# A rotary embedding on one core: the first batch's stores issued later, and one GpSimd product per tile

## The chip, the cores and the metric

The kernel runs on one core of a Trainium2 chip. Times are device microseconds of a whole execution; the profile's span (first to last instruction) is 1.8 to 2.5 us shorter. Engines: DVE is VectorE, POOL is GpSimd, ACT is ScalarE, PE is TensorE, SP issues the loads, ACT also issues the stores. "Transfer engines" are the 16 DMA engines that all loads and stores of the core share.

## The reference

```python
# x: (8, 2048, 8, 64) fp32; cos, sin: (2048, 32) fp32
x1 = x[..., :32]
x2 = x[..., 32:]
out1 = x1 * cos - x2 * sin          # cos, sin broadcast over batch and heads
out2 = x1 * sin + x2 * cos
return np.concatenate([out1, out2], axis=-1)
```

There are 33.55 MB to read, 33.55 MB to write, and 0.52 MB of tables.

## The kernel before

A batch is 4.19 MB. It lies in SBUF as 128 partitions of 8192 values (16 positions of 8 heads of 64), is changed in place and stored. There are five such buffers for eight batches, so batch 5's load waits until batch 0 is stored. A tile is mostly 2048 values per partition, a quarter of a batch.

```python
def store(b, lo, n):
    keep(nc.scalar.dma_start(out=ov[b, :, lo : lo + n], in_=xts[b][:, lo : lo + n]))

for b in range(NBUF):            # 5
    load(b)
# ... identity matrices, nsin = -sin, copies of the tables to PSUM

def rotate(b, lo, n):
    # ... views; kind is "A" (DVE adds), "B" (PE adds), "C" (PE adds, DVE makes both products)
    if kind != "C":
        for u, tab in ((1, sin_sb), (0, nsin)):
            keep(nc.gpsimd.tensor_mul(           # two products per tile, half a tile each
                out=t2u[:, :, u, :].rearrange("p (r h) d -> p r h d", h=H),
                in0=xu[:, :, 1 - u, :].rearrange("p (r h) d -> p r h d", h=H),
                in1=rep(tab[:, r0 : r0 + nr, :], H)))
    keep(nc.vector.tensor_mul(out=t1..., in0=xk, in1=rep(cos_ps[...], 2 * H)))
    if kind == "A":
        keep(nc.vector.tensor_add(out=xt, in0=t1, in1=t2))
    # ... "B", "C": two matmuls with the identity per 512 columns, ACT copies the sum back to xt

for b in range(B):
    # ...
    for lo, n in spans(pieces(b)):
        rotate(b, lo, n)
        # ... once the batch is complete in program order:
                if b == 0:
                    for part in spans([HD, HD, 2 * HD, UNIT, 2 * UNIT]):
                        store(b, *part)          # each waits only for its own tiles
                else:
                    store(b, *whole)
    if b + NBUF <= last:
        load(b + NBUF)
```

Of the kernel before, what the change touches and what calls it, by code (L numbers as in the profile page):

```python
# [9 lines left out]
@with_exitstack  # L10
def kernel(
    ctx: ExitStack,
    tc: tile.TileContext,
    x: bass.AP,
    cos: bass.AP,
    sin: bass.AP,
    out: bass.AP,
):
    nc = tc.nc
    keep = tc.keep_in_program_order  # L20
    f32 = mybir.dt.float32
    PSUM = bass.MemoryType.PSUM

    B, S, H, D = x.shape
    Dh = D // 2
    P = 128
    HD = H * D
    R = S // P
    ROW = R * HD
    UNIT = 4 * HD  # L30
    NBUF = 5
    C = 512
    last = B - 1

    xv = x.rearrange("b (q r) h d -> b q (r h d)", q=P)
    ov = out.rearrange("b (q r) h d -> b q (r h d)", q=P)
    cos_src = cos.rearrange("(q r) d -> q r d", q=P)
    sin_src = sin.rearrange("(q r) d -> q r d", q=P)

    const_pool = ctx.enter_context(tc.tile_pool(name="const", bufs=1))  # L40
    tab_pool = ctx.enter_context(tc.tile_pool(name="tab", bufs=1, space=PSUM))
    t1_pool = ctx.enter_context(tc.tile_pool(name="t1p", bufs=1, space=PSUM))
    o_pool = ctx.enter_context(tc.tile_pool(name="op", bufs=2, space=PSUM))
    t1s_pool = ctx.enter_context(tc.tile_pool(name="t1s", bufs=2))
    xpool = ctx.enter_context(tc.tile_pool(name="xpool", bufs=NBUF))
    t2_pool = ctx.enter_context(tc.tile_pool(name="t2p", bufs=3))

    cos_sb = const_pool.tile([P, R, Dh], f32, tag="cb")
    sin_sb = const_pool.tile([P, R, Dh], f32, tag="sb")
    nsin = const_pool.tile([P, R, Dh], f32, tag="ns")  # L50
    eye = const_pool.tile([P, P], f32, tag="eye")
    neye = const_pool.tile([P, P], f32, tag="neye")
    cos_ps = tab_pool.tile([P, R, Dh], f32, tag="cp")
    sin_ps = tab_pool.tile([P, R, Dh], f32, tag="sp")

    xts = {}

    def spans(sizes):
        lo = 0
        for n in sizes:  # L60
            yield lo, n
            lo += n

    def load(b):
        xt = xpool.tile([P, ROW], f32, tag="xt", name=f"xt{b}")
        for lo, n in spans([UNIT, UNIT, 2 * UNIT] if b == 0 else [ROW]):
            keep(nc.sync.dma_start(out=xt[:, lo : lo + n], in_=xv[b, :, lo : lo + n]))  # L67
            if b == 0 and lo == 0:
                keep(nc.sync.dma_start(out=cos_sb, in_=cos_src))  # L69
                keep(nc.sync.dma_start(out=sin_sb, in_=sin_src))  # L70
        xts[b] = xt

    def store(b, lo, n):
        keep(nc.scalar.dma_start(out=ov[b, :, lo : lo + n], in_=xts[b][:, lo : lo + n]))

    for b in range(NBUF):
        load(b)

    nc.gpsimd.memset(eye, 0.0)  # L79
    nc.gpsimd.affine_select(  # L80
        out=eye,
        in_=eye,
        compare_op=mybir.AluOpType.not_equal,
        fill=1.0,
        base=0,
        pattern=[[-1, P]],
        channel_multiplier=1,
    )
    keep(nc.scalar.mul(nsin, sin_sb, -1.0))  # L89
    keep(nc.scalar.copy(sin_ps, sin_sb))  # L90
    keep(nc.scalar.mul(neye, eye, -1.0))
    keep(nc.vector.tensor_copy(cos_ps, cos_sb))  # L92

    def rep(a, n):
        return dataclasses.replace(a, ap=[a.ap[0][:], a.ap[1][:], [0, n], a.ap[-1][:]])

    kinds = {}
    for b, kind in ((1, "C"), (2, "B"), (3, "C"), (4, "B"), (5, "B")):
        kinds[(b, 0)] = kind

    def rotate(b, lo, n):
        kind = kinds.get((b, lo), "A")
        xt = xts[b][:, lo : lo + n]
        r0 = lo // HD
        nr = n // HD
        xk = xt.rearrange("p (r k d) -> p r k d", r=nr, d=Dh)
        xu = xt.rearrange("p (g u d) -> p g u d", u=2, d=Dh)
        if kind == "A":
            t1 = t1_pool.tile([P, n], f32, tag="t1")
        else:  # L110
            t1 = t1s_pool.tile([P, n], f32, tag="t1s")
        if kind == "C":
            t2 = t1s_pool.tile([P, n], f32, tag="t1s")
        else:
            t2 = t2_pool.tile([P, n], f32, tag="t2")
        t1u = t1.rearrange("p (g u d) -> p g u d", u=2, d=Dh)
        t2u = t2.rearrange("p (g u d) -> p g u d", u=2, d=Dh)
        if kind != "C":
            for u, tab in ((1, sin_sb), (0, nsin)):
                keep(  # L120
                    nc.gpsimd.tensor_mul(  # L121
                        out=t2u[:, :, u, :].rearrange("p (r h) d -> p r h d", h=H),
                        in0=xu[:, :, 1 - u, :].rearrange("p (r h) d -> p r h d", h=H),
                        in1=rep(tab[:, r0 : r0 + nr, :], H),
                    )
                )
        keep(
            nc.vector.tensor_mul(  # L128
                out=t1.rearrange("p (r k d) -> p r k d", r=nr, d=Dh),
                in0=xk,  # L130
                in1=rep(cos_ps[:, r0 : r0 + nr, :], 2 * H),
            )
        )
        if kind == "A":
            keep(nc.vector.tensor_add(out=xt, in0=t1, in1=t2))  # L135
        elif kind == "B":
            for j in range(n // C):
                o = o_pool.tile([P, C], f32, tag="o")
                cs = slice(j * C, (j + 1) * C)
                nc.tensor.matmul(o, eye, t1[:, cs], start=True, stop=False)  # L140
                nc.tensor.matmul(o, eye, t2[:, cs], start=False, stop=True)  # L141
                keep(nc.scalar.copy(xt[:, cs], o))  # L142
        else:
            keep(
                nc.vector.tensor_mul(  # L145
                    out=t2.rearrange("p (r k d) -> p r k d", r=nr, d=Dh),
                    in0=xk,
                    in1=rep(sin_ps[:, r0 : r0 + nr, :], 2 * H),
                )
            )  # L150
            G = C // Dh
            for u in range(2):
                for j in range(n // 2 // C):
                    o = o_pool.tile([P, C], f32, tag="o")
                    gs = slice(j * G, (j + 1) * G)
                    nc.tensor.matmul(o, eye, t1u[:, gs, u, :], start=True, stop=False)  # L156
                    nc.tensor.matmul(  # L157
                        o, eye if u else neye, t2u[:, gs, 1 - u, :], start=False, stop=True
                    )
                    keep(  # L160
                        nc.scalar.copy(  # L161
                            xu[:, gs, u, :], o.rearrange("p (g d) -> p g d", d=Dh)
                        )
                    )

    def pieces(b):
        if b == 0:
            return [2 * HD, 2 * HD, UNIT, UNIT, UNIT]
        if b == last:
            return [UNIT, UNIT, UNIT, 2 * HD, 2 * HD]  # L170
        return [UNIT] * 4

    for b in range(B):
        done = 0
        outs = list(spans([2 * UNIT, UNIT, UNIT] if b == last else [ROW]))
        for lo, n in spans(pieces(b)):
            rotate(b, lo, n)
            done = lo + n
            while outs and sum(outs[0]) <= done:
                whole = outs.pop(0)  # L180
                if b == 0:
                    for part in spans([HD, HD, 2 * HD, UNIT, 2 * UNIT]):
                        store(b, *part)
                else:
                    store(b, *whole)
        if b + NBUF <= last:
            load(b + NBUF)


# [28 lines left out]
```

## Time and profile before

| | before |
|---|---|
| time, median of 6 runs | 163.95 us (163.52 to 164.19) |
| span of the profiled run | 161.9 us |
| DVE, POOL busy | 140.1 us (87%), 139.0 us (86%) |
| moved | 67.6 MB, mean 418 GB/s over the span |
| DVE's last add ends | 152.46 us |

In the page's slice rows each character is one fortieth of the span and its digit the busy share in tenths. The chain of waits follows the last instruction back and attributes the span by engine. The stretches table has the DMA share and GB/s in its last two columns; over a few microseconds its GB/s scatter widely, so for short stretches this text sums single packet records, each packet's bytes spread evenly over its duration. The lines themselves stand in the prediction below.

### The profile page before, as it was taken

The page shows a single profiled execution, that of the slowest core. Times are in us where ns is not written, and L with a number is a line of the kernel's source. Part 1 is how long each engine was busy: PE and PEld are TensorE (multiplying, and loading weights), DVE is VectorE, ACT ScalarE, POOL GpSimd, SP SyncE. Part 2 cuts the span into 40 slices and gives each one's busy share as a digit, 9 for nine tenths or more (in the row PEclk, how much of TensorE's full clock was granted, in tenths as well). Part 3 has the DMA queues.
Part 4 walks back from the last instruction along what each step waited for, and adds up shares of the span by engine and source line. Part 5 has one row for each costly group of instructions (what it writes and reads, how often), then busy time and mean ns, then how long its engine had stood idle before and what let it go on. Part 6 is the DMA issues. An engine that isn't in the chain of part 4 may idle for free.

```text
span 161.9 us, 470 instructions
## 1 busy us (share of the span) xinstructions
PE 46.7 (29%) x80; PEld 18.6 (11%) x80; DVE 140.1 (87%) x66; ACT 14.4 (9%) x24; POOL 139.0 (86%) x70
## 2 busy tenths in 40 slices
PE   0000000498009950893039903970000000000000
PEld 0000000142004310340023402320000000000000
DVE  0468999999999999999999999999999999999600
ACT  3300000014000220041001210130000000000000
POOL 1299999999999899999994999999999999996000
PEclk9999999999955796599755985899555555555555
DMA  5999999999998989998999999989999999999994
GB/s 188 417 435 505 438 413 413 413 421 437 437 470 344 465 364 445 494 413 389 510 397 389 518 391 397 502 389 407 494 397 413 486 397 421 478 397 409 429 417 178
DMA packets 3746, 67.65 MB, mean 418 GB/s; under 512 B 416, under 2 KB 416, under 8 KB 1056
## 3 DMA queue, kind: packets, MB, share of 16 engines
q1 hardware_dynamic: 1728, 34.08, 49.6%
q10 hardware_dynamic: 2016, 33.56, 48.3%
q14 instruction: 2, 0.02, 0.0%
HBM read 34.08 MB, written 33.55 MB: 418 GB/s over the span
## 4 chain that ended last, share of the span: by engine, by line
DVE 75%; POOL 9%; issue 6%; DMA 3%; SPq 0%; DVEq 0%; POOLq 0%
DVE t L128 40%; DVE xt L135 33%; POOL t L121 9%; DMA sin_sb<-in_sin_dram 3%; DVE t L145 3%; DVEq L135 0%; SPq L69 0%; SPq L67 0%; POOLq L121 0%
## 5 line engine op out<-in xcount | busy, mean ns | idle before, releaser
L121 POOL TENSOR_TENSOR t<-xt,sin_sb 128x1024 f32<-128x1024 f32 (+1 forms) x32 | 71.1, 2222 | 8.6 <-DMA sin_sb<-in_sin_dram 5.6
L128 DVE TENSOR_TENSOR t<-xt,cos_ps 128x2048 f32<-128x2048 f32 (+1 forms) x34 | 73.4, 2167 | 0.8
L121 POOL TENSOR_TENSOR t<-xt,nsin 128x1024 f32<-128x1024 f32 (+1 forms) x32 | 71.2, 2225 | 0.0
L135 DVE TENSOR_TENSOR xt<-t,t 128x2048 f32<-128x2048 f32 (+1 forms) x29 | 62.2, 2145 | 5.4 <-POOL t L121 2.5
L140 PE MATMUL o<-t,eye 128*128 128x512 f32 x24 | 17.1, 804 | 25.0 <-DVE t L128 25.0
L156 PE MATMUL o<-t,eye 128*128 128x512 f32 x16 | 10.9, 786 | 36.6 <-DVE t L128 36.6
L141 PE MATMUL o<-t,eye 128*128 128x512 f32 x24 | 15.2, 719 | 0.0
L142 ACT COPY xt<-o 128x512 f32<-128x512 f32 x12 | 7.0, 586 | 46.5 <-PE o L141 46.5
L140 PEld LDWEIGHTS o<-t,eye 128*128 128x128 f32 x24 | 5.6, 250 | 33.4 <-issue 33.4
L161 ACT COPY xt<-o 128x512 f32<-128x512 f32 x8 | 4.7, 586 | 42.7 <-DVE t L128 26.6
L156 PEld LDWEIGHTS o<-t,eye 128*128 128x128 f32 x16 | 3.6, 248 | 41.5 <-POOL t L121 30.4
L141 PEld LDWEIGHTS o<-t,eye 128*128 128x128 f32 x24 | 6.0, 251 | 8.5 <-issue 8.5
L92 DVE COPY cos_ps<-cos_sb 128x512 f32<-128x512 f32 x1 | 0.7, 695 | 6.1 <-DMA cos_sb<-in_cos_dram 6.1
L157 PE MATMUL o<-t,neye 128*128 128x512 f32 x8 | 4.9, 722 | 0.2 <-DVE t L145 0.2
L145 DVE TENSOR_TENSOR t<-xt,sin_ps 128x2048 f32<-128x2048 f32 x2 | 4.6, 2280 | 0.0
L157 PE MATMUL o<-t,eye 128*128 128x512 f32 x8 | 4.1, 592 | 0.0
L157 PEld LDWEIGHTS o<-t,neye 128*128 128x128 f32 x8 | 1.8, 239 | 3.7 <-issue 3.7
L157 PEld LDWEIGHTS o<-t,eye 128*128 128x128 f32 x8 | 1.5, 190 | 1.9 <-issue 1.9
L89 ACT ACT_TABLE_LOAD x1 | 1.3, 1283 | 0.7 <-PEq L202 0.7
L89 ACT ACTIVATE nsin<-sin_sb 128x512 f32<-128x512 f32 x1 | 0.6, 630 | 4.8 <-DMA sin_sb<-in_sin_dram 4.8
L90 ACT COPY sin_ps<-sin_sb 128x512 f32<-128x512 f32 x1 | 0.6, 579 | 0.0
L79 POOL MEMSET eye<- 128x128 f32 x1 | 0.2, 205 | 0.3 <-POOLq L202 0.3
(6 smaller groups left out, 1.0 us busy)
## 6 DMA issues: line engine op xcount, KB each, us to landing
xt<-in_x_dram SPq DMA_DIRECT2D x7, 4096.0 KB, 26.7
out_dram<-xt ACTq DMA_DIRECT2D x6, 4096.0 KB, 33.3
out_dram<-xt ACTq DMA_DIRECT2D x2, 2048.0 KB, 24.3
out_dram<-xt ACTq DMA_DIRECT2D x3, 1024.0 KB, 11.2
xt<-in_x_dram SPq DMA_DIRECT2D x2, 1024.0 KB, 5.9
xt<-in_x_dram SPq DMA_DIRECT2D x1, 2048.0 KB, 11.4
out_dram<-xt ACTq DMA_DIRECT2D x2, 256.0 KB, 18.9
out_dram<-xt ACTq DMA_DIRECT2D x1, 512.0 KB, 32.6
```

What stands on the lines that cost most here:

```text
L89: keep(nc.scalar.mul(nsin, sin_sb, -1.0))
L92: keep(nc.vector.tensor_copy(cos_ps, cos_sb))
L121: nc.gpsimd.tensor_mul(out=t2u[:, :, u, :].rearrange("p (r h) d -> p r h d", h=H), in0=xu[:, :, 1 - u, :].rearrange("p (r h) d -> p r h d" ...
L128: nc.vector.tensor_mul(out=t1.rearrange("p (r k d) -> p r k d", r=nr, d=Dh), in0=xk, in1=rep(cos_ps[:, r0 : r0 + nr, :], 2 * H),)
L135: keep(nc.vector.tensor_add(out=xt, in0=t1, in1=t2))
L140: nc.tensor.matmul(o, eye, t1[:, cs], start=True, stop=False)
L141: nc.tensor.matmul(o, eye, t2[:, cs], start=False, stop=True)
L142: keep(nc.scalar.copy(xt[:, cs], o))
L145: nc.vector.tensor_mul(out=t2.rearrange("p (r k d) -> p r k d", r=nr, d=Dh), in0=xk, in1=rep(sin_ps[:, r0 : r0 + nr, :], 2 * H),)
L156: nc.tensor.matmul(o, eye, t1u[:, gs, u, :], start=True, stop=False)
L157: nc.tensor.matmul(o, eye if u else neye, t2u[:, gs, 1 - u, :], start=False, stop=True)
L161: nc.scalar.copy(xu[:, gs, u, :], o.rearrange("p (g d) -> p g d", d=Dh))
```

## The change

There are two intents. The first batch's stores should not compete with the loads of batches 1 to 4, and POOL should be relieved: one product of a whole tile, through a view that swaps the halves and a table that holds -sin and sin side by side, in place of two products of half a tile. The sine and cosine tables move into a rotating buffer to make room.

```diff
--- before.py
+++ after.py
@@ -45,9 +45,9 @@
     xpool = ctx.enter_context(tc.tile_pool(name="xpool", bufs=NBUF))
     t2_pool = ctx.enter_context(tc.tile_pool(name="t2p", bufs=3))
 
-    cos_sb = const_pool.tile([P, R, Dh], f32, tag="cb")
-    sin_sb = const_pool.tile([P, R, Dh], f32, tag="sb")
-    nsin = const_pool.tile([P, R, Dh], f32, tag="ns")
+    cos_sb = t1s_pool.tile([P, R, Dh], f32, tag="t1s", name="cos_sb")
+    sin_sb = t1s_pool.tile([P, R, Dh], f32, tag="t1s", name="sin_sb")
+    sgn = const_pool.tile([P, R, 2, Dh], f32, tag="sg")
     eye = const_pool.tile([P, P], f32, tag="eye")
     neye = const_pool.tile([P, P], f32, tag="neye")
     cos_ps = tab_pool.tile([P, R, Dh], f32, tag="cp")
@@ -86,13 +86,27 @@
         pattern=[[-1, P]],
         channel_multiplier=1,
     )
-    keep(nc.scalar.mul(nsin, sin_sb, -1.0))
+    for lo, hi in ((0, 4), (4, R)):
+        keep(nc.scalar.mul(sgn[:, lo:hi, 0, :], sin_sb[:, lo:hi, :], -1.0))
+        keep(nc.scalar.copy(sgn[:, lo:hi, 1, :], sin_sb[:, lo:hi, :]))
     keep(nc.scalar.copy(sin_ps, sin_sb))
     keep(nc.scalar.mul(neye, eye, -1.0))
     keep(nc.vector.tensor_copy(cos_ps, cos_sb))
 
     def rep(a, n):
         return dataclasses.replace(a, ap=[a.ap[0][:], a.ap[1][:], [0, n], a.ap[-1][:]])
+
+    def swapped(a, nr):
+        return dataclasses.replace(
+            a,
+            offset=a.offset + Dh,
+            ap=[a.ap[0][:], [HD, nr], [D, H], [-Dh, 2], [1, Dh]],
+        )
+
+    def signed(a, nr):
+        return dataclasses.replace(
+            a, ap=[a.ap[0][:], [D, nr], [0, H], [Dh, 2], [1, Dh]]
+        )
 
     kinds = {}
     for b, kind in ((1, "C"), (2, "B"), (3, "C"), (4, "B"), (5, "B")):
@@ -116,14 +130,13 @@
         t1u = t1.rearrange("p (g u d) -> p g u d", u=2, d=Dh)
         t2u = t2.rearrange("p (g u d) -> p g u d", u=2, d=Dh)
         if kind != "C":
-            for u, tab in ((1, sin_sb), (0, nsin)):
-                keep(
-                    nc.gpsimd.tensor_mul(
-                        out=t2u[:, :, u, :].rearrange("p (r h) d -> p r h d", h=H),
-                        in0=xu[:, :, 1 - u, :].rearrange("p (r h) d -> p r h d", h=H),
-                        in1=rep(tab[:, r0 : r0 + nr, :], H),
-                    )
+            keep(
+                nc.gpsimd.tensor_mul(
+                    out=t2.rearrange("p (r h u d) -> p r h u d", r=nr, h=H, u=2),
+                    in0=swapped(xt, nr),
+                    in1=signed(sgn[:, r0 : r0 + nr, :, :], nr),
                 )
+            )
         keep(
             nc.vector.tensor_mul(
                 out=t1.rearrange("p (r k d) -> p r k d", r=nr, d=Dh),
@@ -178,12 +191,14 @@
             done = lo + n
             while outs and sum(outs[0]) <= done:
                 whole = outs.pop(0)
-                if b == 0:
+                if b == 1:
                     for part in spans([HD, HD, 2 * HD, UNIT, 2 * UNIT]):
-                        store(b, *part)
-                else:
+                        store(0, *part)
+                if b > 0:
                     store(b, *whole)
-        if b + NBUF <= last:
+        if b == 1:
+            load(NBUF)
+        if b > 0 and b + NBUF <= last:
             load(b + NBUF)
```

## The prediction

> **What bounds the kernel now.** I read the page from the top: busy shares, slices, transfer queues, and the chain of waits last, because three things are near their limit at once (DVE, POOL and the DMA engines) and a chain can name only one.
>
> ```profile
> span 161.9 us, 470 instructions
> PE 46.7 (29%) x80; PEld 18.6 (11%) x80; DVE 140.1 (87%) x66; ACT 14.4 (9%) x24; POOL 139.0 (86%) x70
> ...
> DVE  0468999999999999999999999999999999999600
> ...
> POOL 1299999999999899999994999999999999996000
> ...
> DMA  5999999999998989998999999989999999999994
> ...
> HBM read 34.08 MB, written 33.55 MB: 418 GB/s over the span
> ...
> DVE 75%; POOL 9%; issue 6%; DMA 3%; SPq 0%; DVEq 0%; POOLq 0%
> ```
>
> The busy shares (87% and 86%) and the chain (DVE 75%) tempt one to call this a DVE and POOL kernel. The slices say otherwise: the DMA row is the only one that is full from the second slice to the last but one, while DVE and POOL stop some 10 us before the end. So I looked at the end, first in the timeline, then in the table of stretches:
>
> ```profile
> 142.58 10.25 ACTq L74 DMA_DIRECT2D out_dram<-xt  x3
> 151.23 1.23 DVE L135 TENSOR_TENSOR xt<-t,t 128x1024 f32<-128x1024 f32 x1
> 152.49 0.34 ACTq L74 DMA_DIRECT2D out_dram<-xt  x1
> ```
>
> ```profile
> 4.00:37.00 33.00, 6.38 (x10) 2.49 (x11) 28.13 (x15) 2.50 (x5) 30.11 (x16) 1.00 1.03 439
> 37.00:57.00 20.00, 10.92 (x19) 4.42 (x18) 19.48 (x10) 2.37 (x5) 19.53 (x9) 0.74 0.98 411
> 62.00:122.00 60.00, 27.32 (x48) 11.12 (x48) 58.25 (x27) 7.04 (x12) 57.48 (x26) 0.73 1.01 436
> 122.00:158.00 36.00, 0.00 (x0) 0.00 (x0) 29.39 (x15) 0.00 (x0) 26.23 (x14) 0.50 0.99 426
> 158.00:161.90 3.90, 0.00 (x0) 0.00 (x0) 0.00 (x0) 0.00 (x0) 0.00 (x0) 0.50 0.40 170
> ```
>
> The last two columns are the DMA share and GB/s. The last add ends at 152.46 us and the last 1.05 MB store is issued at 152.49, yet the span ends at 161.9. I summed the trace's single packet records (each packet's bytes spread over its duration) to see what the engines did meanwhile: 3.08 MB moved after 152.5, at 429 GB/s. So 3.08 - 1.05 = 2.03 MB of earlier stores stood in the queue ahead of it, worth 2.03 / 0.43 = 4.7 us. The same sums show the rate at 431 to 433 GB/s from 10.6 to 44 us, a dip between 44 and 58 (395 to 430), and again 429 to 433 from 58 to 159. Nothing is left idle: **the kernel is bound by moving 67.6 MB**. Check: 67.6 / 0.432 = 156.5 us, plus 2.2 us until transfers run, plus about 1.3 for slower small packets up to 8 us and the dip, plus 1.9 us from the last packets (160.0) to the end = 161.9.
>
> **What the Trainium skill says.** "DMA: Bandwidth & Descriptors", section "Where 436 GB/s comes from", gives 435.2 GB/s for the 16 ports of a core together; the 432 to 433 here agree, so the rate cannot rise. The same page, "Queues, rings and completion order", says that an engine takes turns between queues packet by packet. The trace agrees: from 20 to 30 us loads moved 4.08 MB and stores 0.24, because a row of a load is 32 KB in one packet and the first store parts have 2 KB and 4 KB packets. "GPSIMD Engine Reference", section 3.1, has 4497 ns for a two-input product of 2048 fp32 elements, and 2293 ns on DVE. DVE agrees (2292 ns). POOL's row here is for 1024 elements:
>
> ```profile
> L121 POOL TENSOR_TENSOR t<-xt,nsin 128x1024 f32<-128x1024 f32 x28 | 66.1, 2360 | 0.0
> L121 POOL TENSOR_TENSOR t<-xt,sin_sb 128x1024 f32<-128x1024 f32 x28 | 66.0, 2356 | 3.1 <-DVE xt L135 2.6
> L135 DVE TENSOR_TENSOR xt<-t,t 128x2048 f32<-128x2048 f32 x25 | 57.3, 2292 | 3.8 <-POOL t L121 1.2 <-DVE t L128 0.4
> ```
>
> Two of these are 4.72 us by their records, but they overlap: in the timeline they start every 2.28 us (18.58, 20.86, 23.15, 25.43), so a pair takes 4.57 us of POOL. Section 7 of that page warns of inner steps over 8 bytes; the new operands keep an inner step of 4 bytes, so nothing there speaks of a penalty.
>
> **The change part by part.**
>
> *One product for two.* POOL goes from 64 products to 32: 28 of 2048 and 4 of 1024 elements, 28 + 2 = 30 tiles' worth. Each replaces 4.57 us by an estimated 4.5 (the skill's figure; the trace has no such instruction), so POOL loses about 30 x 0.07 = 2 us of work. None of it is on the path: DVE needs two passes per ordinary tile, which in the timeline start 4.72 us apart, POOL 4.57, and DVE waited for POOL only 2.5 us in all. Even a shorter DVE chain would not move the end, by the first part. Worth 0 us.
>
> *The table.* ACT now makes four small pieces in place of one 0.63 us negation, and POOL's first product waits for two of them. The 128x128 negation of the identity took 0.30 us, starting 0.5 us after an operation four times as wide, so two 128-column pieces cost about 0.55 us: POOL starts near 7.4 us, not 6.89, and DVE's first add slips by some 0.4 us. DVE's end goes to about 152.9. The slack there is 4.7 us. Worth 0 us.
>
> *The first batch's stores later.* ACT issued five parts (4.19 MB) between 10.66 and 28.5 us. The order of instructions after the change has them behind the four ACT copies of batch 1's first tile, which ended at 40.5 us before. So from 11 to 40 us only loads run. By 40.5 us they have moved some 16.4 MB instead of 15.6, a gain in loads of just the 0.8 MB that stores lose. The fifth load (batch 4) also no longer waits for a store part, but four loads were queued ahead of it. Its end moves from 57.6 to perhaps 54 us.
> The next load (batch 5) waits until all of batch 0 is stored. In both kernels this is when five loads, the tables and one store, 21.5 + 4.2 = 25.7 MB, have moved: 2.2 + 25.7 / 0.43 = 62 us (before: the store was done at 62.7). From there the queues hold the same work in both. All of it comes earlier than DVE needs it: batch 5's load ended at 84.5 and DVE took it up at 97.4. DVE waited for no load of x in batches 1 to 7. What can change is the 0.54 us that the dip from 44 to 58 us cost (0.234 MB missing against 432 GB/s): its small packets now meet other loads. From -0.5 to +0.5 us, centre -0.1.
>
> *Tables in the t1s buffers.* They are read by 9 us; their first reuse is at 28. Worth 0.
>
> Sum: 163.98 + 0 + 0 - 0.1, rounded to **163.8 us**.
>
> **The rivals.**
> 1. *POOL becomes the bound.* The operands now have four free dimensions, one with a negative step, which no instruction of the trace has. POOL would end at 7.4 + 30 x T plus few waits; it ended at 148.2 and DVE 4.2 us later. The end moves once DVE ends later than 152.5 + 4.7 = 157.2, so POOL after 153, or T above 4.85 us (6% over 4.57). At T = 5.2 the time would be some 173 us. Against it: the old operands were already runs of 32 elements with a repeated table, at practically the skill's rate for plain ones. I give it 5%.
> 2. *A dry transfer queue.* Stores held back could leave the engines idle once loads wait for buffers. At about 54 us the loads run out, but then 3.5 MB of batch 0 and 4.2 of batch 1 (issued at 46.7) are queued, 18 us of work, and load 5 enters at 62. Were it wrong, each idle us is a us of time. Under 5%.
> 3. *Engine-bound reading.* If the chain were right (DVE and POOL bound), 2 us off POOL or earlier loads would show as 1 to 3 us: 161 to 163. Against it stand the 2 MB queued when DVE ends.
> 4. *Pure loads run faster than the mix.* 430 GB/s at 8 to 10.6 us against 431.8 after: they don't.
>
> **Range and chances.** The three runs before span 0.7 us. Adding the dip's 0.5 either way: 163.0 to 164.9. Faster by over 2% (below 160.7) would need more than 435 GB/s or the ends to shrink: 1%. Slower by over 2% (above 167.3) is rivals 1 and 2: 6%. Within 2%: 93%.
>
> **What would show it.** Right: DMA full from the second slice to the last but one, mean 416 to 420 GB/s; the last DVE add between 152 and 154 us and the span near 162; POOL's product near 4.5 us; batch 5's load issued at 61 to 63 us. Wrong: a POOL mean above 4.85 us with DVE waiting on it; a DMA slice below 9 inside; or a span under 160 with DVE's last add earlier by as much.

## The result, and the profile after

| | before | after |
|---|---|---|
| time, median of 6 runs | 163.95 us | 164.05 us (163.81 to 164.71) |
| span of the profiled run | 161.9 us | 162.1 us |
| DVE, POOL busy | 140.1, 139.0 us | 140.1, 135.8 us |
| DVE's last add ends | 152.46 us | 153.15 us |
| batch 0 stored; batch 4 loaded (by the bytes moved; the last packet ends up to 0.4 us later) | 62.7; 57.6 us | 63.0; 53.6 us |
| last transfer packet ends | 160.6 us | 160.7 us |

The ratio of after to before is 1.0014, 95% interval 0.9989 to 1.0038.

The page after, the same parts as of before:

```profile
span 162.1 us, 440 instructions
PE 48.0 (30%) x80; PEld 19.3 (12%) x80; DVE 140.1 (86%) x66; ACT 15.1 (9%) x27; POOL 135.8 (84%) x38
...
DVE  0459899999999999999999899999999999999700
...
POOL 1199999999999799999994989999999999994000
...
DMA  5999999999999899998999999999999999999994
...
HBM read 34.08 MB, written 33.55 MB: 417 GB/s over the span
...
DVE 74%; POOL 8%; issue 7%; DMA 3%; SPq 0%; DVEq 0%; ACT 0%
```

POOL is relieved by some 3 us and the span does not move. The DMA row is as full as before (two slices show an 8, four did before); what the engines do under it was rearranged. The groups of POOL and DVE after (count, then busy us and mean ns, then idle us before them and its cause):

```profile
L134 POOL TENSOR_TENSOR t<-xt,sgn 128x2048 f32<-128x2048 f32 x28 | 125.9, 4526 | 5.1 <-DVE xt L148 5.1
L148 DVE TENSOR_TENSOR xt<-t,t 128x2048 f32<-128x2048 f32 x25 | 57.3, 2292 | 3.9 <-DVE t L141 0.9 <-POOL t L134 0.9
```

Start to start, undisturbed whole products are 4.47 to 4.50 us apart, against 4.57 for a pair before. What POOL saves returns as waiting: it idled 5.1 us for DVE, 2.6 before. The end of the timeline after:

```profile
143.27 10.25 ACTq L74 DMA_DIRECT2D out_dram<-xt  x3
...
151.92 1.23 DVE L148 TENSOR_TENSOR xt<-t,t 128x1024 f32<-128x1024 f32 x1
153.18 0.34 ACTq L74 DMA_DIRECT2D out_dram<-xt  x1
```

DVE's end is 0.69 us later than before, and the transfers end at the same time all the same.

### The profile page after: what moved, and what is told of

It is laid out like the page before. It is cut to its first block, busy times and chain, and to the rows that moved or that the text cites. A ratio compares the mean times of both kernels' runs of the same rounds, so it can differ in the third digit from the quotient of the medians.

```text
span 162.1 us, 440 instructions
## 1 busy us (share of the span) xinstructions
PE 48.0 (30%) x80; PEld 19.3 (12%) x80; DVE 140.1 (86%) x66; ACT 15.1 (9%) x27; POOL 135.8 (84%) x38
## 4 chain that ended last, share of the span: by engine, by line
DVE 74%; POOL 8%; issue 7%; DMA 3%; SPq 0%; DVEq 0%; ACT 0%
DVE t L141 40%; DVE xt L148 32%; POOL t L134 8%; DMA sin_sb<-in_sin_dram 3%; DVE t L158 3%; DVEq L148 0%; SPq L69 0%; SPq L67 0%; ACT sgn L90 0%; ACT sgn L91 0%
## 5 line engine op out<-in xcount | busy, mean ns | idle before, releaser
L134 POOL TENSOR_TENSOR t<-xt,sgn 128x2048 f32<-128x2048 f32 (+1 forms) x32 | 135.1, 4253 | 11.4 <-ACT sgn L91 6.3
L170 PE MATMUL o<-t,neye 128*128 128x512 f32 x8 | 6.1, 882 | 0.1
L170 PEld LDWEIGHTS o<-t,neye 128*128 128x128 f32 x8 | 2.5, 329 | 4.8 <-issue 4.8
L90 ACT ACTIVATE sgn<-sin_sb 128x128 f32<-128x128 f32 (+1 forms) x2 | 0.8, 415 | 5.0 <-DMA sin_sb<-in_sin_dram 5.0
L91 ACT COPY sgn<-sin_sb 128x128 f32<-128x128 f32 (+1 forms) x2 | 0.8, 388 | 0.0
```

What stands on the lines that cost most here:

```text
L90: keep(nc.scalar.mul(sgn[:, lo:hi, 0, :], sin_sb[:, lo:hi, :], -1.0))
L91: keep(nc.scalar.copy(sgn[:, lo:hi, 1, :], sin_sb[:, lo:hi, :]))
L134: nc.gpsimd.tensor_mul(out=t2.rearrange("p (r h u d) -> p r h u d", r=nr, h=H, u=2), in0=swapped(xt, nr), in1=signed(sgn[:, r0 : r0 + nr, ...
L170: nc.tensor.matmul(o, eye if u else neye, t2u[:, gs, 1 - u, :], start=False, stop=True)
```

## The experiments

Theory T: moving the bytes binds, and DVE's end has some 4 us to spare. Rival D: the DVE and POOL chain, which carries 82 to 84% of the chain of waits (DVE alone 74 to 75%), binds.

### More work on DVE: e1 and e2

The changed kernel with a cosine product of batch 6 made a second time, for one tile (e1) or all four (e2); the results stay right.

```diff
+        if b == 6 and lo // UNIT in (1,):        # e2: (0, 1, 2, 3)
+            keep(nc.vector.tensor_mul(out=t1..., in0=xk, in1=rep(cos_ps[...], 2 * H)))
         if kind == "A":
```

e1, one more product:

> The changed kernel with one of DVE's cosine products of batch 6 made twice (2.3 us more DVE work, same result). Theory T (transfers bind, DVE's end has some 4 us to spare): last add ends near 155.4 us instead of 153.15, span and time stay within 0.4 us of the changed kernel (164.05). Rival D (the DVE and POOL chain binds): time 2.3 us up, 166.3.

e2, four more:

> The changed kernel with all four cosine products of batch 6 made twice (9.2 us more DVE work). T: last add near 162.3 us; the stores ahead of the last one would be drained by 157.6 (160.0 less 2.4 for 1.05 MB), so 4.4 us of the 9.2 are hidden and the rest shows, plus 0 to 2 us for starting on an empty queue: time 168.8 to 171. D: all 9.2 us show, 173.3.

Measured: e1 164.10 us (163.92 to 164.58), ratio to before 1.0012 (0.9957 to 1.0066); e2 169.08 us (168.97 to 169.14), ratio 1.031. The timelines' ends, e1 first, then e2:

```profile
154.12 1.22 DVE L156 TENSOR_TENSOR xt<-t,t 128x1024 f32<-128x1024 f32 x1
155.38 0.34 ACTq L74 DMA_DIRECT2D out_dram<-xt  x1
```

```profile
152.34 10.25 ACTq L74 DMA_DIRECT2D out_dram<-xt  x3
...
160.99 1.22 DVE L156 TENSOR_TENSOR xt<-t,t 128x1024 f32<-128x1024 f32 x1
```

In e1 DVE ends 2.2 us later than in the changed kernel and the time does not follow. In e2 it ends at 162.21, 9.06 us later, and the time rises by 5.0 (over e1's of the same rounds, too): 4.1 us were hidden, about the 4.4 expected. D, which wanted 2.3 and 9.2 us, falls. The stretches of e2 show the spare time used up: from 140 to 144 us, while batch 6 was still being worked on, the queue ran dry. In the packet records it was empty once more from 161 to 163 us, before the last store.

```profile
130.00:140.00 10.00, 0.00 (x0) 0.00 (x0) 9.79 (x5) 0.00 (x0) 9.34 (x3) 0.50 0.97 419
140.00:144.00 4.00, 0.00 (x0) 0.00 (x0) 3.86 (x3) 0.00 (x0) 1.45 (x2) 0.50 0.33 139
```

### Fewer bytes: e3, e4 and e5

e3 is the changed kernel without the last quarter of batch 4's store, e4 without all of it; e5 is the kernel before without all of it. Their results are wrong in the places not stored.

```diff
# e3
+                if b == 4:
+                    store(b, 0, 3 * UNIT)
-                if b > 0:
+                elif b > 0:
                     store(b, *whole)
# e4
-                if b > 0:
+                if b > 0 and b != 4:
                     store(b, *whole)
# e5
-                else:
+                elif b != 4:
                     store(b, *whole)
```

e3, 1.05 MB less:

> The changed kernel without the last quarter of batch 4's store (1.05 MB less; result wrong on purpose in that quarter). T: 1.05 MB at 432 GB/s is 2.4 us: time 161.6, and DVE's last add stays at 153.1. D: no change, 164.0.

e4, 4.19 MB less, changed kernel:

> The changed kernel without batch 4's store (4.19 MB less; result wrong on purpose in that batch). T: 9.7 us of transfer vanish, but then the last store waits for DVE's end at 153.1 us, so only the spare 4 us less 0 to 1.5 us for an empty queue are gained: time 160 to 162, bound by DVE now. D: no change, 164.0.

e5, 4.19 MB less, kernel before:

> The kernel before without batch 4's store, to see the change where DVE binds. T: DVE's last add ends at 152.5 us here and 0.7 us later with the change, so this is 0.7 us (0.4 to 1.0) faster than the changed kernel without that store: 159.3 to 161.3. D, with POOL's 2 us on the path: the changed one is up to 2 us faster.

Measured: e3 161.63 us, 2.42 below the changed kernel's 164.05 and 2.37 below e6 (164.00, next section but one), which ran on the same chip in the same rounds, as 1.05 MB at 432 GB/s would have it. e4 160.16 (159.72 to 160.34) and e5 159.39 (159.19 to 159.57), same chip and rounds. Without the 4.19 MB only about 4 us are gained in place of 9.7, because then DVE is the bound. The DMA rows of e4 and, second, e5 show the holes:

```profile
DMA  5999999999999999999999999999999990997946
```

```profile
DMA  5999999999999999999999999999999990997946
```

And here, where the engines' work does count, the change costs: the medians differ by 0.77 us, and DVE's last add ends at 153.26 us in e4 and 152.55 in e5, 0.71 later (its line in e4, then in e5):

```profile
152.03 1.23 DVE L148 TENSOR_TENSOR xt<-t,t 128x1024 f32<-128x1024 f32 x1
```

```profile
151.32 1.23 DVE L135 TENSOR_TENSOR xt<-t,t 128x1024 f32<-128x1024 f32 x1
```

POOL's shorter work gives nothing even then, since DVE waited for POOL hardly at all after the start (in the changed kernel 2.7 us in all, 2.5 of them in batch 0); the later start of POOL comes through to DVE's end in full. The first instructions, before and then after, show where it begins (start us, duration us):

```profile
6.77 0.63 ACT L89 ACTIVATE nsin<-sin_sb 128x512 f32<-128x512 f32 x1 [4.75 <-DMA sin_sb<-in_sin_dram]
...
6.89 1.26 POOL L121 TENSOR_TENSOR t<-xt,sin_sb 128x512 f32<-128x512 f32 x1 [5.58 <-DMA sin_sb<-in_sin_dram]
```

```profile
7.03 0.31 ACT L90 ACTIVATE sgn<-sin_sb 128x128 f32<-128x128 f32 x1 [5.02 <-DMA sin_sb<-in_sin_dram]
7.25 0.28 ACT L91 COPY sgn<-sin_sb 128x128 f32<-128x128 f32 x1
...
7.61 2.35 POOL L134 TENSOR_TENSOR t<-xt,sgn 128x1024 f32<-128x1024 f32 x1 [6.31 <-ACT sgn L91]
```

Before, POOL began with the sine as it came from memory; after, it waits for two pieces from ACT and starts 0.72 us later. Of this 0.26 us is the sine landing later in that run. In all 14 traces POOL begins 0.12 us after ACT's first work on the sine with two products, and 0.58 with one: the new table costs 0.46 us. That work itself begins between 6.77 and 7.13 us, whichever kernel runs, and this scatter is the rest (7.13 in e4 and 6.87 in e5: again 0.26). What makes up the rest of the 0.77 between the medians is not shown.

### The parts one by one: e6 and e7

e6 is the kernel before with the later stores alone, e7 with the single product and its table alone (each takes its half of the diff above).

e6, stores late:

> The kernel before with only the later issue of batch 0's stores. T: the queues hold the same work from 63 us on; 163.7 to 164.4, ratio to before 0.998 to 1.003, batch 0 stored at 62.5 to 63.2 us; the dip in the rate around 50 to 56 us costs 0.6 to 0.8 us in place of 0.54. D: no change either, or up to 1 us faster if earlier loads feed DVE.

e7, one product:

> The kernel before with only the single product per tile and its table; stores as before. T: POOL busy 135 us in place of 139, DVE's last add 0.5 to 0.9 us later than before (the table), all hidden: ratio 0.998 to 1.002, some 163.9 us. D: 1 to 2 us faster from POOL's shorter work, or 0.7 us slower from the later DVE end.

Measured: e6 164.00 us (163.93 to 164.10), ratio 1.0001 (0.9949 to 1.0054), batch 0 stored at 63.1 us: as expected, but for the dip from 44 to 58 us, which cost 0.9 us and not 0.6 to 0.8. e7 165.70 us (165.20 to 166.53), ratio 1.0093 (1.0047 to 1.0138): expected by neither theory, though its DVE ended at 153.05, well within the spare time.

### The first store whole: e8

```diff
-                    for part in spans([HD, HD, 2 * HD, UNIT, 2 * UNIT]):
-                        store(0, *part)
+                    store(0, 0, ROW)
```

> The changed kernel with batch 0's store as one transfer of 32 KB rows in place of five parts with rows of 2 to 16 KB. T1 (the small packets make the dip around 50 to 56 us): the dip of 0.75 us shrinks below 0.3, time 163.5 (0.3 to 0.7 us less). T2 (the dip comes from the loads ending on some engines before others): the dip and the time stay, 164.0.

Measured: 165.20 us (164.69 to 165.52), ratio 1.0055 (1.0011 to 1.0099), about 1.1 us slower than the changed kernel where 0.3 to 0.7 faster or nothing was expected. Both of its theories missed.

### The slow stretches: e7 and e8 again, beside e6 and the changed kernel

The packet records of e7 and e8 have all 16 engines occupied in the dips (a sum of durations of 15.9 to 16.2 us per us). What differs is the duration of single packets of 32 KB: 1.21 us otherwise, 1.24 to 2.5 us there. To see whether that was chance, the four kernels were run again unchanged on another chip.

The changed kernel:

> The changed kernel itself, again, beside the next three. The earlier runs of single parts gave 165.7 (product alone) and 165.2 (first store whole) where 164 was expected. In their traces all 16 engines stay occupied, but in stretches of 3 to 5 us some 32 KB packets take 1.4 to 2.4 us in place of 1.21. If those stretches belong to that chip or session, this kernel too is at 165 to 166 here; if they belong to the kernels, it is at 164.0 to 164.3.

The product alone:

> The product alone, again. S (slow stretches belong to this kernel's timing): 165.2 to 166.5 again, with stretches near 66 to 70 and 116 to 121 us as before and a tail on a few engines after 160. C (chance of session or chip): 163.7 to 164.5, or stretches at other times.

The first store whole:

> The changed kernel with batch 0's store whole, again. S: 164.7 to 165.5, stretches near 42 to 45 and 76 to 80 us. C: 163.5 to 164.3, or stretches at other times.

The late stores alone:

> The late stores alone, again, in the same session as the three above: 163.8 to 164.3 under S, 0.5 to 2 us more if the session slows everything.

Measured: e9 164.03 us (163.87 to 164.24), ratio 1.0016; e12 164.01 (163.83 to 164.57), ratio 1.0021; e10 164.56 (164.08 to 166.33), ratio 1.0088 (1.0040 to 1.0135); e11 165.82 (165.20 to 166.27), ratio 1.012 (1.0089 to 1.0151). Below, the "lost" column is how much less was moved from 10 to 158 us than 432.5 GB/s would have moved, in us of that rate; the "excess" column sums, over 32 KB packets longer than 1.24 us, what they took over 1.213 us, and divides by 16 engines.

| profiled run | span us | lost us | excess us | stretches under 400 GB/s (us, whole microseconds) |
|---|---|---|---|---|
| before | 161.9 | 0.65 | 0.60 | 55 to 57 |
| after | 162.1 | 0.90 | 0.80 | 50 to 54 |
| e9, changed again | 162.0 | 0.84 | 0.75 | 50 to 54 |
| e6, stores late | 162.2 | 1.25 | 1.14 | 50 to 54, 77 to 79 |
| e12, stores late again | 162.0 | 1.00 | 0.91 | 51 to 54 |
| e7, one product | 164.6 | 1.91 | 1.86 | 56 to 58, 66 to 70, 79 to 80, 117 to 120 |
| e10, one product again | 162.2 | 1.02 | 0.98 | 56 to 58, 67 to 69 |
| e8, store whole | 162.8 | 1.72 | 1.80 | 43 to 46, 68 to 69, 77 to 80 |
| e11, store whole again | 163.2 | 1.85 | 1.90 | 43 to 46, 76 to 80 |

The excess accounts for nearly all that was lost in each run, so slow packets, not idle engines, make these dips. They lie at nearly the same places when a kernel is repeated on another chip (e8 and e11; the one at 50 to 54 us in e6 and e12), so they belong to the kernel and not to the chip; that answers for S in e11, which is even 0.3 us above its range. e8 differs from the changed kernel in the form of one store alone, so there the arrangement of the transfers moves them; for e7 this is argued, not shown. For e10 S holds only in part: four of its six runs are at 164.1 to 164.7 and two at 166.2 to 166.3, the profiled one being of the short kind, without the stretch at 117.

In the long profile of e7 the end is uneven too: after 160 us only 5 to 6 engines were still moving, until 163.3. The records name no engine, but they can be laid end to end, each packet where another ended, and then form 16 chains (a reconstruction). From 65.7 to 70.4 us six chains of e7 have two packets each of 1.47 to 2.43 us, while the other ten stay at 1.21. This fits the uneven end: e7's last packet ended 2.7 us after that of the kernel before, with only 1.26 us more lost on the average of 16 engines. That the same engines are late in both places is not shown. The kernel before has runs as long as that of e10 at times: 5 of its 36 runs were above 165 us, and none of the 26 runs of the kernels with late stores in parts (after, e1, e6, e9, e12), which lie between 163.81 and 164.71.

What makes those packets slow is not settled: the records name no engine and no address. Small packets are not needed for it (T1 of e8): in e8 and e11 the stretch at 50 to 54 us is gone (433 GB/s), but the one at 43 to 46 us (326 and 325 GB/s) has data packets of 32 KB alone. Whether small packets play a part at 50 to 54 us is not shown. Nor did loads that end early on some engines begin that stretch (T2): in the chains of the changed kernel slow packets start at 50.2 us, and the first engine runs out of loads at 53.3.

No run points to a kernel that beats both: every version that moves all 67.6 MB had a median of 164.0 us or more, and the kernel before 163.6 to 164.1 in the four sets of rounds. In the three sets where both ran, the medians with late stores in parts are 0.1 to 0.4 us above it (for example 164.03 and 164.01 against 163.61), in the direction of the 0.2 to 0.6 us more that their profiles lost; the ratios' intervals all include 1, so a small cost of the late stores is likely, but not shown.

## Why the prediction was right

- **The bound.** Transfers bind: shown by e3 (1.05 MB less, 2.42 us less) and e1 (2.2 us more DVE, nothing). The spare time of DVE's end, put at 4.7 us before, and at 4.4 after the change, was 4.1 in e2. The working's check of the span took 160.0 us for the last packets; the trace has the last one at 160.6, so the sum agrees in part by that choice.
- **One product for two.** 4.5 us was estimated, 4.48 measured (the skill's figure, cited there for a product, is the page's for an add; the two agree here). In the company of the late stores it is worth 0 as said, and rival 1 (above 4.85 us) is gone: a negative step and four dimensions cost nothing visible.
- **The table.** The mechanism was right and so was its size: counted from the sine's arrival, POOL starts 0.46 us later and DVE ends 0.44 later, where some 0.5 and 0.4 were predicted. DVE's end slipped by 0.69 us because the sine also landed 0.26 later in that run, which is chance. Hidden; e4 against e5 shows that it counts where DVE binds.
- **Later stores.** Batch 4's load ended at 53.6 us (54 predicted), batch 0 was stored at 63.0 (62), and batch 5's load was issued at 63.7, just beyond the 61 to 63 given. From 10 to 40 us the loads gained 0.8 MB, as worked out. The first store packet came at 45.0 and not near 40.5, because it left 3.7 us after its issue at 41.3; this changed nothing. Rival 2 (a dry queue) did not occur.
- **The dip.** This was the only term with a size, -0.1 us, and its sign was wrong: in the profiled runs the loss from 44 to 58 us grew from 0.54 to 0.76 us, and over the run from 0.65 to 0.90, within the stated half microsecond. The cause named for it, small packets that meet loads, is not needed for such a stretch (e8, e11); it stays open.
- **Luck.** The prediction made each part worth 0 by itself. The product alone cost 0.9% on two chips (e7 165.70 us, above the whole stated range; e10 164.56), in stretches of slow packets for which the prediction has no term. Beside the late stores this did not happen. Why not is open, and that the sum came out is in so far luck.
- **Signs and sums.** The sign of being wrong "a DMA slice below 9 inside" was badly set: two slices show an 8, and the kernel before had four. The sum 163.98 - 0.1 is 163.88, which rounds to 163.9, not 163.8.
- **Rival 3** (the chain is right) is refuted by e1. Rival 4 was right not to be taken: pure loads ran at 432 to 433 GB/s.

The prediction's 163.8 us and the measured 164.05 differ by less than the runs of one kernel among themselves.

## What to carry to other kernels

Before speeding up the engine that leads the chain of waits, look at what still stands in the transfer queue when that engine ends: here 2 MB, worth 4.7 us, so a faster DVE could gain nothing, and one slower by 2.2 us cost nothing (e1). Holding stores back moves no byte away; it reorders the queue, and where a later load waits for a store, the sum of bytes up to that point sets the time in both orders (62.7 and 63.0 us here). The order is not free, though: one store in another form cost 1.8 us in the same rounds (e11 165.82 us, e9 164.03). A transfer-bound kernel is tested most cheaply by leaving out a known number of bytes and by doing one instruction twice.

## What the Trainium skill lacked or had wrong

- "DMA: Bandwidth & Descriptors", section "Where 436 GB/s comes from": 432 to 433 GB/s held for a mix of loads and stores too, close to its 435.2. What I found on no page: stretches of 1 to 5 us in which 32 KB packets take 1.24 to 2.5 us in place of 1.21 with all 16 engines occupied; they cost 0.65 to 1.9 us per run, and their places belong to the kernel.
- The same page, "Specifications", gives a first-byte latency of about 0.6 us for this issue path. With loads queued on the same engines the first store packet came 3.7 us after the issue (after) and 3.9 us (before, 10.66 to 14.57); with nothing queued yet the first load packet came 1.0 us after (0.74 to 1.73).
- "DMA: Bandwidth & Descriptors", section "Where 436 GB/s comes from", also says that for transfers between HBM and SBUF the HBM side, some 358 GB/s, binds. It did not here: this one-core program moved 417 to 418 GB/s on average over the span and 432 to 433 in its full stretches. ("Perfetto Trace Analysis", sections "Engine Utilization" and "Roofline", too takes 358 GB/s as 100%, but says that a core alone can reach about 120%; this one is at 117%.)
- "GPSIMD Engine Reference", section 3.1: its 4497 ns (for an add) agrees with 4.48 us start to start for this product, while the records say 4526 ns. It has no figure for operands of four dimensions with a negative step; here they cost nothing on top.
